# Recurrence units of four and three chunks cut at the dense groups, attention blocks counted by themselves

## The chip, the cores and the metric

The kernel runs on one core of one Trainium2 chip. The metric is the device time of one execution in microseconds (us). TensorE (PE) does the matrix products, PEld is its weight load, VectorE is DVE, ScalarE is ACT, GpSimd is POOL, and SyncE (SP) issues nearly all transfers. One profiled execution shows every instruction, its place in time and what ended the wait before it.

## What is computed

One layer of a decoder trunk runs over a prompt of 2048 tokens and 64 sample tokens, with model width 1024, all in float32. Cut to what matters:

```python
hn = rms_norm(x, g_pre_mix);  proj = hn @ w_in            # q, k, v of attention; r, k, v, decay, a, gate of RWKV
o_attn = sliding-window attention (window 128, 8 q heads, 2 kv heads, sinks)
def step(S, inp):                                         # RWKV-7, one token after the other
    sa = einsum('bhij,bhj->bhi', S, kk_t)
    S = S * w_t - sa (kk_t * a_t) + v_t k_t
    return S, einsum('bhij,bhj->bhi', S, r_t)
y = group_norm(ys) + bonus;  o_rw = y * g
mix = concat([o_attn, o_rw]) @ w_out;  x = x + rms_norm(mix)
f = (silu(conv3(z)) * u) @ w_ffn_out  with  z, u = rms_norm(x) @ w_ffn_in;  x = x + rms_norm(f)
```

## The kernel before

**Dense work.** The 2112 tokens are cut into five groups of columns: 448, 448, 448, 448 and 320 (`groups`, `GW`). For each group g there are stages: `P[g]` (`project`, 20 weight tiles), `O[g]` (`outproj`, 8 tiles) and two for the ConvFFN (`ffn`: 60 tiles, then a last one of 6), which stand in the list `F` as `F[2g]` and `F[2g+1]`. A tile's work is called a task here. It is 24 matmuls, since each product is made from two halves of either operand: `xhi·wh`, `xlo·wh`, `xhi·wl` (L182). For each task ACT writes `wh` (L351) and DVE writes `wl` (L352) out of the weight tile `w`. The stages run in the order of the list `order`:

P0 P1 P2 O0 P3 F0 O1 F1 P4 F2 O2 F3 O3 F4 F5 O4 F6 F7 F8 F9

**Side work.** Norms, the element-wise part of the projection (`shift`, `pair`, `rotary`) and what follows a stage (`rest`, L835 to L844 and L939 to L941) are generators. They are stepped between dense matmuls.

**Mixer.** The recurrence is done in chunks of 64 tokens (32 of them), the attention in blocks of 128 tokens (16 of them). A unit (`Mixer.unit`) is four chunks and two blocks, 256 tokens, so there are eight, and one more for the sample tokens. The recurrence of a unit goes through these steps:

- `scores`: for each chunk the matmuls `sc_e`, `sc_o`, and two DVE products with a mask (L1003) that make the tile `G`;
- `invert`: 31 steps on DVE, two instructions each (L1041, L1042), on all chunks of the unit at once (16 partitions to a chunk). Then an ACT copy (L1045), two stores that SP issues (L1050 is one), loads, and the matmuls `pz`;
- `chain`: chunk after chunk the matmuls `vt`, `bkt`, `pc`, `pu`, `pS`, with the state carried on;
- `groupnorm` on tiles of two chunks, `finish` (`pt`, `pg`), and the store of the result.

The attention of a unit (`attend`) runs beside it: `sc` and L1266, softmax (L1230 to L1241), `ppt`, `po`.

**What sets the order.** `Flow` keeps a planned clock that each emitted matmul moves on. After each dense matmul group `tick` lets at most one side step and one mixer step follow. A unit has a window from `start` to `end` in planned dense time; while the mixer's planned cost so far is over its share of `UNIT` (48e3), it is not stepped. A stage whose condition is not met is forced: `force` steps sides and mixer, without dense work between, until it is. `O[g]` needs the recurrence and attention of all units that touch its tokens: with groups of 448 and units of 256, `O0` needs units 0 and 1 (512 tokens), `O1` four units, `O2` six, `O3` seven. All engines take their instructions in the order in which they were emitted.

## Time and profile before

| | us |
|---|---|
| median of three runs | 2909.87 (2905.41 to 2914.93) |
| the profiled execution, its own time | 2909.42 |
| span of the profiled execution | 2907.6 |
| PE busy in the span | 2772.0 |
| DVE busy in the span | 1925.0 |
| ACT busy in the span | 1409.1 |

The dense stages can be found in time by counting matmuls of `gm` and `pf`. P1 runs from 126.7 to 315.2 us, P2 to 513.6, O0 to 572.0, P3 to 748.1, F0 to 1149.2, O1 to 1188.9, F1 to 1247.4, P4 to 1350.7, F2 to 1746.1, O2 to 1790.4, F3 to 1835.1, O3 to 1890.6, F4 to 2261.8. No mixer work stands after F4. The granted clock has two values in this trace, 1.0 (2.4 GHz) and 0.5 (1.2 GHz) of full speed, so a stretch's mean tells how much of it ran at the lower one.

### The profile page before, as it was taken

Reading aid. Unit: us, or ns where it says so; the run is one execution under the profiler, and the core shown is the slowest. Engines: PE = TensorE matmul, PEld = TensorE weight load, DVE = VectorE, ACT = ScalarE, POOL = GpSimd, SP = SyncE. Lnnn points to the kernel's source line nnn. Section 1 sums busy time; section 2 is a strip of 40 time slices with the busy share of each in tenths; the row PEclk is TensorE's granted clock in tenths of the full one; section 3 lists DMA queues with packets and bytes.
Section 4 is the critical chain, followed back from the end, with each engine's and each line's share of the span. In section 5 each row is a group of like instructions: output and inputs, shape, how many; then the busy total and the mean of one; then the engine's idle time right before and its main releaser. Section 6 shows DMA issues by size and latency. Waiting matters only on the chain.

```text
span 2907.6 us, 46258 instructions
## 1 busy us (share of the span) xinstructions
PE 2772.0 (95%) x16993; PEld 2354.7 (81%) x16993; DVE 1925.0 (66%) x3792; ACT 1409.1 (48%) x2628; POOL 239.3 (8%) x519
## 2 busy tenths in 40 slices
PE   8997998989999999998999999899999999999997
PEld 6875776758778789776887898778989999999997
DVE  6884885686756655687665556965764764447666
ACT  6553545546564554454655434455333443334543
POOL 1010010010000000022000010000000001001111
PEclk9997999989999999998999999999999999999998
DMA  6665645746744343565544335664433553335443
GB/s 200 195 201 136 193 142 147 219 127 196 217 143 126 104 148 123 170 198 142 180 134 136 115 108 160 208 196 133 130 115 109 186 182 107 109 105 177 157 150 119
DMA packets 310529, 446.58 MB, mean 154 GB/s; under 512 B 118536, under 2 KB 238952, under 8 KB 310288
## 3 DMA queue, kind: packets, MB, share of 16 engines
q1 hardware_dynamic: 309872, 443.48, 49.5%
...
q14 instruction: 91, 0.75, 0.1%
q10 hardware_dynamic: 432, 0.16, 0.0%
HBM read 362.19 MB, written 76.97 MB: 151 GB/s over the span
## 4 chain that ended last, share of the span: by engine, by line
PE 75%; DVE 13%; DMA 5%; ACT 3%; issue 3%; SPq 1%; DVEq 0%; ACTq 0%
PE gm L182 46%; PE pf L182 16%; PE pc L182 3%; DVE wl L352 2%; PE po L182 2%; DVE tt L1042 1%; DVE tmp L1041 1%; PE pz L182 1%; PE ppt L186 1%; ACT wh L351 1%; PE sc L182 1%; PE pu L182 1%; DMA w<-in_w_all 1%; PE pS L182 1%; PE sc_e L182 1%
## 5 line engine op out<-in xcount | busy, mean ns | idle before, releaser
L182 PE MATMUL gm<-xhi,wh 128*128 128x448 f32 (+3 forms) x2880 | 1056.1, 369 | 44.2 <-ACT wh L351 18.9
L182 PE MATMUL gm<-xhi,wl 128*128 128x448 f32 (+3 forms) x2880 | 1042.1, 363 | 14.9 <-DVE wl L352 14.6
L182 PE MATMUL gm<-xlo,wh 128*128 128x448 f32 (+3 forms) x2880 | 1039.5, 362 | 4.5 <-DVE xlo L352 4.2
L351 ACT CAST wh<-w 128x1024 fp32r<-128x1024 f32 (+1 forms) x470 | 489.5, 1042 | 720.3 <-PE gm L182 332.8
L352 DVE TENSOR_TENSOR wl<-w,wh 128x1024 fp32r<-128x1024 f32 (+1 forms) x470 | 569.9, 1213 | 381.8 <-ACT wh L351 377.6
L182 PEld LDWEIGHTS gm<-xhi,wh 128*128 128x128 f32 (+2 forms) x2880 | 544.2, 189 | 131.4 <-issue 31.4
L182 PEld LDWEIGHTS gm<-xhi,wl 128*128 128x128 f32 (+2 forms) x2880 | 544.3, 189 | 73.6 <-DVE wl L352 21.0
L182 PEld LDWEIGHTS gm<-xlo,wh 128*128 128x128 f32 (+2 forms) x2880 | 545.3, 189 | 60.3 <-DVE xlo L352 10.6
L182 PE MATMUL pf<-hh,wh 128*128 128x448 f32 (+1 forms) x880 | 317.8, 361 | 3.8 <-DVE acc L908 2.9
L182 PE MATMUL pf<-hl,wh 128*128 128x448 f32 (+1 forms) x880 | 312.5, 355 | 0.6 <-DVE hl L352 0.6
L182 PE MATMUL pf<-hh,wl 128*128 128x448 f32 (+1 forms) x880 | 312.4, 355 | 0.2 <-DVE wl L352 0.2
L881 POOL COPY zcar<-zz 128x2 f32<-128x2 f32 x110 | 74.4, 676 | 1547.6 <-ACT zz L870 1547.6
L908 DVE TENSOR_TENSOR acc<-acc,pf 128x448 f32<-128x448 f32 (+1 forms) x200 | 117.3, 589 | 103.4 <-PE pf L182 102.7
L182 PEld LDWEIGHTS pf<-hh,wh 128*128 128x128 f32 x880 | 165.3, 188 | 23.6 <-DVE acc L908 4.9
L182 PEld LDWEIGHTS pf<-hh,wl 128*128 128x128 f32 x880 | 165.3, 188 | 12.7 <-issue 1.0
L182 PEld LDWEIGHTS pf<-hl,wh 128*128 128x128 f32 x880 | 165.5, 188 | 11.8 <-DVE hl L352 1.0
L877 DVE SCALAR_TENSOR_TENSOR c<-zz,c_cw,c 128x448 f32<-128x448 f32 (+1 forms) x220 | 140.8, 640 | 26.2 <-ACT c L871 24.1
L891 DVE TENSOR_TENSOR c<-c,gm 128x448 f32<-128x448 f32 (+1 forms) x110 | 65.0, 591 | 120.4 <-PE gm L182 94.3
L884 ACT ACTIVATE c<-c 128x448 f32<-128x448 f32 (+1 forms) x110 | 61.2, 557 | 126.5 <-DVE c L877 89.3
L1041 DVE TENSOR_TENSOR tmp<-gb,tt 64x31 f32<-64x31 f32 (+21 forms) x279 | 91.4, 328 | 3.6 <-DMA gb<-dgr 1.0
L1042 DVE TENSOR_TENSOR tt<-tt,tmp 64x31 f32<-64x31 f32 (+21 forms) x279 | 91.9, 329 | 2.8
L351 ACT CAST xhi<-r 128x448 fp32r<-128x448 f32 (+1 forms) x112 | 59.3, 542 | 70.8 <-DMA r<-od 25.8
...
## 6 DMA issues: line engine op xcount, KB each, us to landing
w<-in_w SPq DMA_DIRECT2D x220, 512.0 KB
...
```

The lines of the kernel that those rows point to most:

```text
L182: return self.te.matmul(out, lhsT, rhs, **kw)
L186: return self.te.transpose(*args)
L351: self.nc.scalar.copy(out=hi, in_=src)
L352: self.nc.vector.tensor_tensor(out=lo, in0=src, in1=hi.bitcast(F32), op=ALU.subtract)
L877: v.scalar_tensor_tensor(out=c[:, :npr], in0=z[:, j:j + npr], scalar=cw(j), in1=c[:, :npr], op0=ALU.mult, op1=ALU.add)
L881: nc.gpsimd.tensor_copy(out=sh.zcar[:, f, :], in_=z[:, npr:npr + 2])
L884: nc.scalar.activation(out=c, in_=c, func=AF.Silu)
L891: v.tensor_tensor(out=c, in0=c, in1=ps, op=ALU.mult)
L908: v.tensor_tensor(out=accs[c], in0=accs[c], in1=ps, op=ALU.add)
L1041: v.tensor_tensor(out=tm, in0=col, in1=row, op=ALU.mult)
L1042: v.tensor_tensor(out=tt[:nb, w:, 0:w], in0=tt[:nb, w:, 0:w], in1=tm, op=ALU.subtract)
```

## The change

The prompt's recurrence is cut into nine units of 4, 3, 4, 3, 4, 3, 4, 4 and 3 chunks, so that units end at chunks 7, 14 and 21, which are the ends of the dense groups 0, 1 and 2. (The end of group 3, chunk 28, lies inside the eighth unit.) The attention blocks go with the units as 2, 2, 2, 1, 2, 2, 2, 1, 2, and each block has a token of its own: `O[g]` now needs the units that begin before its end and the blocks up to it. The `need` of a step is worked out from its own last token: attention block 3 waits for P1, while the unit of chunks 4 to 6 waits for P0 alone. The planned cost of a unit is `CHUNK` a chunk and `BLOCK` a block in place of `UNIT`, and the starts of the windows are moved. Three chunks leave a last tile of 64 rows in `chain`, `groupnorm` and `finish`.

```diff
-UNIT = 48e3
+CHUNK, BLOCK, SAMPLE = 7.3e3, 9.3e3, 48e3
...
-            if self.mixed - m0 > UNIT * (self.clock.t - self.mixed - start) / max(end - start, 1.0):
+            if self.mixed - m0 > cost * (self.clock.t - self.mixed - start) / max(end - start, 1.0):
...
-    def chain(self, c0, Gs, ys):
+    def chain(self, c0, n, Gs, ys):
...
-        for c in range(NC_):
+        for c in range(n):
             if c % 2 == 0:
+                m = min(2, n - c)
...
-    def unit(self, u, need):
+    def unit(self, u, c0, n, blocks, need):
...
         def attention():
-            yield lambda: need <= self.done
-            yield from self.attend(NB * u)
-            yield from self.attend(NB * u + 1)
-            self.flow.post(lambda: self.done.add(("A", u)))
+            for b in blocks:
+                w = need(128 * (b + 1))
+                yield lambda: w <= self.done
+                yield from self.attend(b)
+                self.flow.post(lambda b=b: self.done.add(("A", b)))
 
         def recurrence():
-            yield lambda: need <= self.done
+            w = need(CH * (c0 + n))
+            yield lambda: w <= self.done
...
+UNITS = [(4, 2), (3, 2), (4, 2), (3, 1), (4, 2), (3, 2), (4, 2), (4, 1), (3, 2)]
...
-        O = [dn.outproj(g, {(x, u) for u in range(-(-ends[g] // T)) for x in "AR"} | ({("S", 0)} if gs[g][2] else set())) for g in range(ng)]
+        O = [dn.outproj(g, {("R", u) for u, (c0, _, _) in enumerate(units) if CH * c0 < ends[g]} | {("A", b) for b in range(-(-ends[g] // 128))}
+                        | ({("S", 0)} if gs[g][2] else set())) for g in range(ng)]
...
-        windows = [(f(P[1], 0), f(P[1], 1)), (f(P[2], 0), f(P[2], 0.9)), (f(P[3], 0.1), f(F[0], 0.15)), (f(F[0], 0.15), f(F[0], 0.53)),
-                   (f(F[0], 0.53), f(F[0], 0.93)), (f(F[2], 0), f(F[2], 0.47)), (f(F[2], 0.47), f(F[2], 0.93)), (f(F[4], 0), f(F[4], 0.5))]
...
-        flow.units.append((f(F[4], 0.5), f(F[4], 0.93), [mx.sample({("P", ng - 1)})]))
+        starts = [f(*x) for x in ((P[1], 0), (P[1], 0.75), (P[2], 0.6), (P[3], 0.4), (F[0], 0.15), (F[0], 0.5), (F[2], 0), (F[2], 0.35),
+                                  (F[2], 0.7))]
+        need = lambda t: {("P", g) for g in range(ng) if gs[g][0] < t}
+        for u, (x, y, (c0, n, bs)) in enumerate(zip(starts, starts[1:] + [f(F[4], 0.35)], units)):
+            flow.units.append((x, y, CHUNK * n + BLOCK * len(bs), mx.unit(u, c0, n, bs, need)))
+        flow.units.append((f(F[4], 0.35), f(F[4], 0.9), SAMPLE, [mx.sample({("P", ng - 1)})]))
```

**First place: PE, the last tasks of P2.** The rows are the kernel before; `gm` is a dense matmul, `pt` and `pg` are the `finish` of unit 1, `sc` is attention of unit 2.

```order
L182 MATMUL gm<-xlo,wh 128x448
L182 MATMUL gm<-xhi,wl 128x448
L182 MATMUL pb<-b_4964,c_blockones 128x448
L186 MATMUL pt<-c_ident,y 128x128
L182 MATMUL pg<-sg,c_g_up 128x256 x2
L186 MATMUL pt<-c_ident,y 128x128 x7
L182 MATMUL pg<-sg,c_g_up 128x256 x2
L182 MATMUL sc<-kx,q 128x256 x4
L182 MATMUL gm<-xhi,wh 128x448 x2
```

The kernel after has the two halves of that `finish` apart; these are the rows around the first half, PE, in the last task but one of P2.

```order
L182 MATMUL gm<-xlo,wh 128x448
L182 MATMUL gm<-xhi,wl 128x448
L186 MATMUL pt<-c_ident,y 128x128
L182 MATMUL pg<-sg,c_g_up 128x192 x2
L182 MATMUL gm<-xhi,wh 128x448
```

Before, both halves stand between two dense matmuls of the 20th task, in which the chain of unit 1 also ends; now that chain ends in the 17th task, the first half stands in the 19th and the second in the 20th, and 30 dense matmuls lie between the halves.

**Second place: DVE, the middle of O3.** The rows are the kernel before; `acc` is the `rest` of F3, `tmp` and `tt` are the inversion of unit 7, `m`, `nm`, `es`, `den` its softmax, `wl` a weight half that the dense matmuls of O3 need.

```order
L939 SCALAR_TENSOR_TENSOR acc<-acc,c_gT,rb 128x448
L1041 TENSOR_TENSOR tmp<-gb,tt 64x252
L941 TENSOR_TENSOR acc<-acc,r 128x448
L1042 TENSOR_TENSOR tt<-tt,tmp 64x18x14
L1232 TENSOR_SCALAR nm<-m 128x4
L1233 TENSOR_TENSOR es<-c_sink,m 128x4
L1041 TENSOR_TENSOR tmp<-gb,tt 64x255
L769 TENSOR_TENSOR sa<-sa,sq 128x448
L1042 TENSOR_TENSOR tt<-tt,tmp 64x17x15
L352 TENSOR_TENSOR wl<-w,wh 128x1024
```

The kernel after, DVE, the same end of that `rest` in O3.

```order
L941 TENSOR_TENSOR acc<-acc,r 128x448
L939 SCALAR_TENSOR_TENSOR acc<-acc,c_gT,rb 128x448
L941 TENSOR_TENSOR acc<-acc,r 128x448
L769 TENSOR_TENSOR sa<-sa,sq 128x448
L941 TENSOR_TENSOR acc<-acc,r 128x448
L352 TENSOR_TENSOR wl<-w,wh 128x1024
```

Before, all 31 inversion steps of unit 7 stand in O3 and the first two tasks of F4; now the last prompt unit's stand in F2 (the 45th to the 51st of 60 tasks), and O3 has none.

**Third place: DVE, the middle of P3.** The rows are the kernel before; `L`, `b` and `tha` are the projection's `pair`, `s` and `G` are attention and scores of unit 3.

```order
L712 TENSOR_SCALAR L<-L 128x448
L713 SCALAR_TENSOR_TENSOR L<-scanm,L 128x448
L1266 SCALAR_TENSOR_TENSOR s<-sc,c_amask 128x512 x2
L728 SCALAR_TENSOR_TENSOR b_7486<-tha,e_7487 128x448
L1003 TENSOR_TENSOR G<-sc_e,c_wkmask 128x4x128
L1003 TENSOR_TENSOR G<-sc_o,c_wkmask 128x4x128
```

The kernel after, DVE, in the second half of P3.

```order
L1041 TENSOR_TENSOR tmp<-gb,tt 48x207
L677 SCALAR_TENSOR_TENSOR v<-h,c_vec,hm 128x448
L1042 TENSOR_TENSOR tt<-tt,tmp 48x23x9
L712 TENSOR_SCALAR L<-L 128x448
L1041 TENSOR_TENSOR tmp<-gb,tt 48x220
L713 SCALAR_TENSOR_TENSOR L<-scanm,L 128x448
L1042 TENSOR_TENSOR tt<-tt,tmp 48x22x10
```

Before, the inversion of unit 2 stands in the first seven tasks of P3, among the `rest` of O0; now unit 2's stands from the fifth task of O0 to the second of P3, and the one that shares P3's second half with the pairs is unit 3's, of three chunks (48 partitions), from the 14th task of P3 to the third of F0.

## Rows read from the trace of the kernel before

**Rows 1.** The page's first part: busy us, share of the span, instructions.

```profile
PE 2772.0 (95%) x16993; PEld 2354.7 (81%) x16993; DVE 1925.0 (66%) x3792; ACT 1409.1 (48%) x2628; POOL 239.3 (8%) x519
```

**Rows 2.** Windows: start:end, width, busy PE, PEld, DVE, ACT, POOL, clock, DMA, GB/s.

```profile
226.00:283.00 57.00, 40.26 (x324) 29.46 (x323) 25.01 (x52) 22.90 (x48) 1.80 (x8) 0.73 0.48 126
384.70:431.00 46.30, 43.57 (x205) 35.36 (x204) 44.98 (x117) 21.03 (x45) 7.60 (x12) 1.00 0.45 132
483.30:523.20 39.90, 28.78 (x128) 19.71 (x129) 26.21 (x62) 15.39 (x28) 1.99 (x5) 0.70 0.59 174
521.00:636.00 115.00, 96.72 (x485) 77.87 (x484) 92.19 (x232) 59.80 (x135) 6.01 (x13) 0.93 0.61 182
748.10:1149.20 401.10, 396.30 (x2680) 330.16 (x2679) 246.86 (x507) 206.39 (x388) 28.70 (x47) 1.00 0.44 135
1188.90:1247.40 58.50, 45.94 (x232) 37.88 (x230) 52.04 (x121) 26.63 (x65) 0.31 (x2) 0.91 0.62 196
1247.40:1386.30 138.90, 123.84 (x775) 101.54 (x776) 104.56 (x258) 70.65 (x164) 32.15 (x65) 0.90 0.59 171
1790.40:1835.10 44.70, 43.43 (x241) 34.10 (x239) 43.47 (x103) 22.40 (x46) 1.10 (x2) 1.00 0.62 191
1835.10:1953.80 118.70, 106.99 (x707) 84.49 (x706) 94.49 (x226) 62.92 (x128) 3.75 (x5) 0.91 0.62 197
2322.00:2622.30 300.30, 299.58 (x1461) 271.88 (x1462) 164.28 (x241) 122.47 (x178) 25.83 (x43) 1.00 0.40 128
```

**Rows 3.** Timeline of PE in P3: dense matmuls on either side of a clock change.

```profile
611.33 0.57 PE L182 MATMUL gm<-xhi,wh 128*96 128x448 f32 x1
611.70 0.57 PE L182 MATMUL gm<-xlo,wh 128*96 128x448 f32 x1
...
612.69 0.36 PE L182 MATMUL gm<-xlo,wh 128*96 128x448 f32 x1
612.89 0.36 PE L182 MATMUL gm<-xhi,wl 128*96 128x448 f32 x1
```

**Rows 4.** Timeline of PE at the end of P2.

```profile
497.36 1.83 PE L182 MATMUL pb<-b,c_blockones 128*128 128x448 f32 x2 [5.36 <-DVE rsg L53]
...
503.24 0.90 PE L186 MATMUL pt<-c_ident,y 128*128 128x128 f32 x3 [1.02 <-DVE y L1194]
```

**Rows 5.** Timeline of DVE in O3.

```profile
1872.97 0.67 DVE L939 SCALAR_TENSOR_TENSOR acc<-acc,c_gT,rb 128x448 f32<-128x448 f32 x1
1873.56 0.40 DVE L1041 TENSOR_TENSOR tmp<-gb,tt 64x252 f32<-64x252 f32 x1
...
1876.11 1.21 DVE L352 TENSOR_TENSOR wl<-w,wh 128x1024 fp32r<-128x1024 f32 x1
```

**Rows 6.** Timeline of PE at the same moment.

```profile
1877.37 0.74 PE L182 MATMUL gm<-xhi,wl 128*128 128x448 f32 x1 [7.42 <-DVE wl L352]
```

**Rows 7.** Groups on DVE: line, form, count, busy us, mean ns, idle before.

```profile
L1041 DVE TENSOR_TENSOR tmp<-gb,tt 64x31 f32<-64x31 f32 (+21 forms) x279 | 91.4, 328 | 3.6 <-DMA gb<-dgr 1.0
L1042 DVE TENSOR_TENSOR tt<-tt,tmp 64x31 f32<-64x31 f32 (+21 forms) x279 | 91.9, 329 | 2.8
L1003 DVE TENSOR_TENSOR G<-sc_e,c_wkmask 128x512 f32<-128x512 f32 x32 | 21.8, 682 | 8.8 <-PE sc_o L182 6.6 <-PE sc_e L182 2.1
L1230 DVE TENSOR_REDUCE m<-s 128x4 f32<-128x1024 f32 (+1 forms) x32 | 37.6, 1174 | 0.1
L1266 DVE SCALAR_TENSOR_TENSOR s<-sc,c_amask 128x512 f32<-128x512 f32 (+1 forms) x64 | 41.4, 662 | 13.5 <-PE sc L182 13.5
```

**Rows 8.** Waits of SP at an inversion's end: total us, times, longest.

```profile
SPq L1050 <- DVE tt L1042: 23.9, 8, 17.8
```

**Rows 9.** Waits of ACT at an inversion's end: the same columns.

```profile
ACT gb L1045 <- DVE tt L1042: 14.3, 5, 7.9
```

**Rows 10.** Groups on PE of the transposes of `finish` and `chain`.

```profile
L186 PE MATMUL pt<-c_ident,y 128*128 128x128 f32 x64 | 12.0, 297 | 3.6 <-DVE y L1194 2.4 <-ACT fin L1214 1.1
L186 PE MATMUL vt<-c_ident,vl 128*128 128x128 f32 x64 | 11.1, 299 | 0.0
```

More of the change, by code (lines that the diff above doesn't have):

```diff
@@ L239, in mixer @@
         if not self.mix and self.units:
-            start, end, gens = self.units[0]
+            start, end, cost, gens = self.units[0]
             if self.clock.t - self.mixed >= start or now == math.inf:
@@ L243, in mixer @@
                 self.mix = [Stream(g) for g in gens]
-                self.span = max(start, self.clock.t - self.mixed), end, self.mixed
+                self.span = max(start, self.clock.t - self.mixed), end, self.mixed, cost
         ready = [s for s in self.mix if s.at <= now and s.cond()]
@@ L259, in tick @@
         if self.mix:
-            start, end, m0 = self.span
-            if self.mixed - m0 > UNIT * (self.clock.t - self.mixed - start) / max(end - start, 1.0):
+            start, end, m0, cost = self.span
+            if self.mixed - m0 > cost * (self.clock.t - self.mixed - start) / max(end - start, 1.0):
                 return
@@ L1142, in chain @@
         yield 5000
-        for c in range(NC_):
+        for c in range(n):
             if c % 2 == 0:
+                m = min(2, n - c)
                 pv = self.ps("vt")
                 for p in range(4):
-                    te.transpose(pv[:, 128 * p:128 * p + 128], V[:, p], sh.ident)
-                for i in range(2):
+                    te.transpose(pv[:CH * m, 128 * p:128 * p + 128], V[:, p, :CH * m], sh.ident)
+                for i in range(m):
                     uvs[c + i] = self.t2("uv", tag="uv", bufs=2)
@@ L1154, in chain @@
             yield 1500
-            if c + 1 < NC_:
+            if c + 1 < n:
                 nxt = self.factors(c0 + c + 1)
@@ L1290, in attend @@
             yield 1000
-    def unit(self, u, need):
-        sh, nc, a = self.sh, self.nc, self.a
-        c0 = NC_ * u
+    def unit(self, u, c0, n, blocks, need):
+        sh, a = self.sh, self.a
         def attention():
-            yield lambda: need <= self.done
-            yield from self.attend(NB * u)
-            yield from self.attend(NB * u + 1)
-            self.flow.post(lambda: self.done.add(("A", u)))
+            for b in blocks:
[3 more added lines that the diff above has]
+                self.flow.post(lambda b=b: self.done.add(("A", b)))
         def recurrence():
-            yield lambda: need <= self.done
+            w = need(CH * (c0 + n))
+            yield lambda: w <= self.done
             Gs, ys = [], []
-            for c in range(NC_):
+            for c in range(n):
                 yield from self.scores(c0 + c, sh.wkmask, Gs)
             yield from self.invert(Gs)
-            yield from self.chain(c0, Gs, ys)
-            for y in ys:
-                yield from self.groupnorm(y)
-            yield from self.finish(ys, T, T * u)
-            if c0 + NC_ == sh.nch:
+            yield from self.chain(c0, n, Gs, ys)
+            for i, y in enumerate(ys):
+                yield from self.groupnorm(y, min(128, CH * n - 128 * i))
+            yield from self.finish(ys, CH * n, CH * c0)
+            if c0 + n == sh.nch:
                 self.store(a["o_wkv"], sh.S[self.si])
@@ L1621, in program @@
             sh.stacks(lambda name: mx.b4([128, D], name, "G"))
-        gs, nu = groups(seq), seq // T
+        gs = groups(seq)
         ng = len(gs)
@@ L1626, in program @@
         ends = [min(t0 + n, seq) for t0, n, _ in gs]
-        O = [dn.outproj(g, {(x, u) for u in range(-(-ends[g] // T)) for x in "AR"} | ({("S", 0)} if gs[g][2] else set())) for g in range(ng)]
+        units = []
+        for n, bs in UNITS:
+            c0, b0 = (units[-1][0] + units[-1][1], units[-1][2][-1] + 1) if units else (0, 0)
+            units.append((c0, n, range(b0, b0 + bs)))
+        O = [dn.outproj(g, {("R", u) for u, (c0, _, _) in enumerate(units) if CH * c0 < ends[g]} | {("A", b) for b in range(-(-ends[g] // 128))}
+                        | ({("S", 0)} if gs[g][2] else set())) for g in range(ng)]
         F = [f for g in range(ng) for f in dn.ffn(g)]
@@ L1635, in program @@
         f = lambda s, x: at[id(s)][0] + x * s.cost()
-        windows = [(f(P[1], 0), f(P[1], 1)), (f(P[2], 0), f(P[2], 0.9)), (f(P[3], 0.1), f(F[0], 0.15)), (f(F[0], 0.15), f(F[0], 0.53)),
-                   (f(F[0], 0.53), f(F[0], 0.93)), (f(F[2], 0), f(F[2], 0.47)), (f(F[2], 0.47), f(F[2], 0.93)), (f(F[4], 0), f(F[4], 0.5))]
-        for u, (x, y) in enumerate(windows):
-            need = {("P", g) for g in range(ng) if gs[g][0] < T * (u + 1)}
-            flow.units.append((x, y, mx.unit(u, need)))
-        flow.units.append((f(F[4], 0.5), f(F[4], 0.93), [mx.sample({("P", ng - 1)})]))
+        starts = [f(*x) for x in ((P[1], 0), (P[1], 0.75), (P[2], 0.6), (P[3], 0.4), (F[0], 0.15), (F[0], 0.5), (F[2], 0), (F[2], 0.35),
[4 more added lines that the diff above has]
+        flow.units.append((f(F[4], 0.35), f(F[4], 0.9), SAMPLE, [mx.sample({("P", ng - 1)})]))
         flow.run(dn.run(order))
```

4 lines of the change are left out of this document (2 added, 2 removed).

## The prediction, made before the changed kernel ran

> **What bounds the kernel now.** I read the page's busy times first. PE is busy for 2772.0 of 2907.6 us, DVE for 1925.0, ACT for 1409.1 [rows 1], so PE sets the time, and only 135.6 us of it are idle. But a busy PE can be a slow one. In P3 the same dense matmuls follow each other every 0.37 us (611.33, 611.70) and a moment later every 0.20 us (612.69, 612.89) [rows 3]; the first two ran at the lower clock of 1.2 GHz. So I price a stretch's loss as its idle time of PE plus (1 - granted clock) times its width: the time at the lower level is twice (1 - clock) of the width, and about half of it would be saved at the higher one. By the windows [rows 2], each cut at dense tasks, that gives
>
> - u0: 226.0 to 283.0, P1, end of unit 0's inversion: 16.7 + 0.27 x 57 = 32.1
> - A: 483.3 to 523.2, last task of P2 to the second of O0: 11.1 + 0.30 x 39.9 = 23.1
> - B: 521.0 to 636.0, O0 to the seventh task of P3: 18.3 + 0.07 x 115 = 26.3
> - C: 1188.9 to 1247.4, F1: 12.6 + 0.09 x 58.5 = 17.8
> - D: 1247.4 to 1386.3, P4 and two tasks of F2: 15.1 + 0.10 x 138.9 = 29.0
> - E: 1835.1 to 1953.8, O3 and the first tasks of F4: 11.7 + 0.09 x 118.7 = 22.4
>
> The six hold 151 us. F0, with two whole units mixed in, loses 4.8 us in 401, and F6, with none, 0.7 in 300 [rows 2]. So the amount of mixer work costs little beyond its own time on PE; what costs is where it meets side work on DVE, ACT and SP.
>
> Next I read who ends the waits. In A, PE stands 5.36 and 1.02 us behind small DVE instructions of the group norm [rows 4], because O0 is forced and nothing dense lies between. In E, inversion steps alternate with the `rest` of F3, and a `wl` behind them arrives 7.42 us late for PE [rows 5, 6]. At the end of an inversion, ACT and SP wait in line with it: SP up to 17.8 us before the store L1050, ACT up to 7.9 before the copy L1045, 14.3 in five cases [rows 8, 9]; weight loads and `wh` queue behind them.
>
> DVE being nearly full is not itself a loss: F3 has DVE busy 43.5 of 44.7 us and loses 1.3; the stretch of unit 1's inversion, 384.7 to 431.0, has 45.0 of 46.3 and loses 2.7 [rows 2]. It becomes one when DVE gets more than PE in the same tasks, or many inversion steps at once.
>
> **The change part by part.** I counted in both orders what stands in each dense task and priced it with the group means; sums of many small groups below are such estimates.
>
> *Work added.* One more inversion: 62 DVE instructions, (91.4 + 91.9) / 9 = 20.4 us, as a step's price is that of its columns [rows 7]. It falls into F2, where like F0 (DVE 247 of 401 us) there is room, so I put it at nothing; without that cover it costs up to 20. On PE the tiles of 64 rows bring 16 more `pt` and 16 more `vt` records, at 12.0 / 64 and 11.1 / 64 us [rows 10] at most 5.8, at least 0 where they overlap neighbours; I take **+3**.
>
> *A, end of P2.* O0 needs chunks to 7 in place of 8. Unit 1 starts in the same place, but its chain ends three tasks earlier and the two halves of its `finish` get dense work between. Between the 17th task of P2 and the second of O0, PE has some 12 us less (chain matmuls) and DVE some 12 more: unit 2's scores, softmax and two splits come in. DVE is late next, by about 7 us over PE. So of 23.1 between 7 and all remain; I take 10, the lower end with a little of the group norm's chain: **-13** (-16 to 0).
>
> *B, O0 and P3.* Unit 2's inversion moves from among O0's `rest` in P3 into O0, where DVE had room, and its chain (PE work, some 24 us) comes to stand beside that `rest`. DVE gets about 5 us more in B, 97 in all, while PE's work goes from 97 to 121, so PE leads. Unit 1's row says 3 may remain, B itself 26; I take 14: **-12** (-23 to 0).
>
> *E, O3.* The inversion, a block's softmax and scores leave, a chunk and a half and two group norms come: DVE -18, PE -10. DVE then has about 77 us beside some 97 of PE. Nearest is F3, which loses 1.3; with the group norm's small steps now inside O3 I take 8 of 22.4: **-14** (-21 to -5).
>
> *D, P4.* Unit 6 stands where unit 5 stood, but all its scores, and one block's attention more, now fall into P4: six more L1003, four L1266, two L1230 [rows 7] are 4.1 + 2.6 + 2.3, and half a `pair` comes in, 15 us of DVE in all, with 9 of PE that have left F4. DVE leads, so the stretch grows by up to 15, of which 9 are moved, not new: **+6** (-5 to +15).
>
> *End of P3 and F0.* Unit 3's inversion now meets the projection's pairs. The rows nearest are unit 0's and unit 1's, both among pairs: 32.1 and 2.7. Unit 0 has 13 of its 31 steps in one dense task, unit 1 two to five a task in the second half; unit 3 has two to five. So I take unit 1's side: **+4** (2 to 32).
>
> *C, F1.* The next stage waits for the norm of P4, which waits for the `rest` of O1; no unit is involved, so the force stays. Unit 5's chain adds 2 us of DVE: **+2** (-5 to +8). Its PE work fills idle time that is there in both. O1, O2, F2 take over what F4 loses, at PE's price: 0.
>
> *u0.* The same instructions stand there, 14 steps in the one task for 13: 0 (-10 to +5). After F4 nothing differs.
>
> A side look at the price of a loss. In E, PE is busy for 90% of the width, its weight load for 84.49 of 118.7 us; in F6 for 271.88 of 300.3 [rows 2]. The Trainium skill, Perfetto Trace Analysis, "Identifying the Most-Contended Engine", says that matmul busy time is no measure of the distance to the limit, and to take the share of weight loads. With F6's share of 0.905 as full, A, B and E lose 18.1 + 29.0 + 25.3 = 72.4, against 71.8 by my price and 41.1 by idle time alone. By that rule the sum stays; by idle alone the three gains shrink to about 22 us and the time is 2902.
>
> **Sum.** -13 - 12 - 14 + 6 + 4 + 2 + 3 = **-24 us**. The profiled execution took 2909.42 us, 1.8 over its span, and stands within 0.5 of the median of 2909.87. So 2909.9 - 24 = **2886**.
>
> **The rivals.**
>
> - *The inversion blocks ACT and SP among the pairs (slower).* Unit 3's inversion at the end of P3 and unit 6's in P4, with eight steps in P4's last task, hold up `wh` and the weight loads as unit 0's does. Price: the end of P3 costs 32 in place of 4, D 15 in place of 6, so -24 + 28 + 9 = +13: 2923. It decides from the point where SP waits longer than some 10 us at L1050, as it does once now (17.8), and PE for `wh`. For it: the largest of the six losses is of this kind. Against: unit 1 does the same work among pairs for 2.7.
> - *Waits of latency, not of load (no change).* A's and E's small chains are as long as before and only stand elsewhere: unit 1's group norm before O0, unit 8's inside O3, the `rest` of O0 before F0. Then A gives 5, B 4, E 7, and the additions of 15 stay: -1, 2909. For it: DVE gains 20 us in all, and P2 and P4 get more of it. Against: between the halves there is now dense work, and 30 matmuls at 0.20 us cover 6 us, more than the 5.36 of the worst wait.
> - *The additions are hidden (larger gain).* D, C and the end of P3 at nothing: -39 + 3 = -36, 2874. With A, B and E near their lower ends too it would be below 2860.
>
> **How the numbers follow.** I give the forecast 0.48, the hidden additions 0.14, the waits of latency 0.21, the blocked queues 0.17. Faster means below 2901, since about 0.3% is what a measurement of this kernel can tell from no change; the first two cases are there but for their edges, where a gain shrinks to a few us: 0.62. Within 0.3%: the third: 0.22. Slower: 0.16. The range takes in the hidden additions with half of what A, B and E could still give, and most of the case of no change: 2862 to 2914. The blocked queues and the far low end are left out.
>
> **What the changed kernel's profile would show.** Right: at the end of P2 no wait of 5 us behind `rsg` and a clock near 1; in O3 no `tmp`, `tt`, and no `wl` 7 us late; the first seven tasks of P3 at a clock above 0.9. P4 longer than 103.3 us by 5 to 15, F4 shorter by some 30. Wrong: a wait of PE for `wh` at the end of P3 or of P4 with SP standing before L1050; F1 longer than 65 us; O0 stretched by unit 2's inversion, so that B only moves forward; u0 changed by more than 10 us, which would mean that small differences in order decide and not the loads counted here.

## The result and the profile after

The kernel after takes 2894.47 us (median of 11 runs, 2889.23 to 2902.03), the kernel before beside it 2910.14 us. The ratio is 0.9944, with a 95% interval of 0.9934 to 0.9954: 15.7 us faster. The forecast was 24 us, 2886 us, with a range of 2862 to 2914. The sign and the range hold, the gain is two thirds of the forecast.

The profiled execution of after took 2902.03 us, the longest of its 11 runs. Its difference to the profile of before (7.4 us) is therefore smaller than that of the medians, and a few us in one stage are not to be read from the two traces alone. That is why steps A, B and E are also tested by runs that undo them.

The page's first part of after, to be read beside [rows 1]: the added inversion is 62 of the 100 instructions that DVE has more (3892 for 3792), and PE is busy for 6.1 us more.

```profile
PE 2778.1 (96%) x17017; PEld 2375.4 (82%) x17017; DVE 1954.9 (67%) x3892; ACT 1413.9 (49%) x2635; POOL 266.2 (9%) x521
```

The windows of after, cut at the same dense tasks as [rows 2] (start:end, width, busy PE, PEld, DVE, ACT, POOL, granted clock, DMA share, GB/s). In order: u0, A, B, F0, C, D, E.

```profile
229.20:292.50 63.30, 44.33 (x392) 31.27 (x391) 26.20 (x54) 25.22 (x55) 2.68 (x6) 0.76 0.52 141
490.65:525.47 34.82, 26.46 (x116) 19.40 (x115) 28.77 (x62) 15.31 (x40) 2.03 (x1) 0.81 0.74 222
525.47:664.42 138.95, 129.35 (x935) 98.99 (x934) 96.86 (x232) 78.89 (x178) 6.69 (x15) 0.90 0.61 186
751.20:1152.40 401.20, 395.79 (x2679) 332.07 (x2679) 259.01 (x536) 209.65 (x395) 37.95 (x49) 0.99 0.45 135
1199.90:1261.00 61.10, 47.79 (x304) 39.10 (x302) 52.25 (x141) 28.23 (x65) 0.31 (x2) 0.85 0.58 184
1261.00:1412.10 151.10, 136.75 (x877) 109.79 (x876) 118.49 (x290) 78.58 (x187) 29.31 (x69) 0.91 0.59 175
1862.30:1948.50 86.20, 85.28 (x539) 73.45 (x539) 76.66 (x164) 50.56 (x92) 5.49 (x13) 1.00 0.68 220
```

With the price of the prediction, PE's idle time plus (1 - clock) times the width:

| stretch | before | forecast change | after | change read |
|---|---|---|---|---|
| u0 | 32.1 | 0 | 34.2 | +2.1 |
| A | 23.1 | -13 | 15.0 | -8.1 |
| B | 26.3 | -12 | 23.5 | -2.8 |
| end of P3 and F0 (F0's loss) | 4.8 | +4 | 9.4 | +4.6 |
| C | 17.8 | +2 | 22.5 | +4.7 |
| D | 29.0 | +6 | 28.0 | -1.0 |
| E | 22.4 | -14 | 0.9 | -21.5 |

The changes add up to -22, with PE's 6 us of further busy time -16. That this lies beside the -15.7 of the medians is chance. The table is read from two executions that differ by 7.4 us, PE's 6 us hold time at the lower clock, which the price has already counted, and outside the seven stretches the price rose. Two places show it, before and then after: from u0 to A, and from the end of E to the end of F4.

```profile
283.00:483.30 200.30, 192.33 (x1395) 145.31 (x1393) 144.37 (x315) 106.80 (x233) 17.57 (x38) 0.98 0.57 166
1953.80:2261.80 308.00, 307.94 (x1835) 270.89 (x1834) 190.24 (x339) 131.09 (x214) 25.02 (x49) 1.00 0.40 125
```

```profile
292.50:490.65 198.15, 189.15 (x1244) 146.10 (x1243) 146.39 (x340) 107.39 (x228) 25.64 (x44) 0.95 0.54 154
1948.50:2256.30 307.80, 304.82 (x1664) 269.44 (x1663) 181.74 (x315) 122.36 (x192) 24.46 (x41) 0.98 0.40 122
```

Between u0 and A the loss goes from 12.0 to 18.9, in F4 from 0.1 to 9.1. In the whole span the price falls by about 2 us only (PE's idle time from 135.6 to 122.2, the mean clock from 0.973 to 0.969). The first of the two places belongs to step A: the chain of unit 1, which now ends earlier, stands in P2 from 445.5 to 463.1 us without a dense matmul, and the clock is at 0.5 from 453.9 to 467.6. So from the end of u0 to the second task of O0 PE loses 33.9 for 35.1: nearly all that A gains is lost just ahead of it.

In the table B stands out: forecast as the second largest gain, it gave nearly nothing, though PE leads there as foreseen (129 us busy beside DVE's 97). Half of what B loses is clock: 10.2 us at 0.5 between O0 and P3, with waits of 2.17 and 2.48 us for the norm, and 17.1 us in P3.

What happens in P3 is seen in PE's timeline in task 3 of P3 (start, us, engine, line, operation, count, idle time before and what ended it):

```profile
612.93 1.07 PE L182 MATMUL po<-pT,va 128*64 128x512 f32 x2 [0.31 <-ACT pT L1280]
...
615.40 0.72 PE L182 MATMUL pz<-G,zt 32*32 32x32 f32 x16 [0.86 <-ACT zt L1071]
616.04 0.66 PE L186 MATMUL vt<-c_ident,vl 128*128 128x128 f32 x4
...
617.58 1.80 PE L182 MATMUL pc<-S,ab 64*128 64x64 f32 x14
619.31 1.12 PE L182 MATMUL pc<-uv,G 64*64 64x64 f32 x16
620.88 1.51 PE L182 MATMUL pu<-rhs,G 64*64 64x64 f32 x16 [0.45 <-ACT rhs L1111]
...
629.76 1.51 PE L182 MATMUL pu<-rhs,G 64*64 64x64 f32 x16 [0.45 <-ACT rhs L1111]
631.23 0.74 PE L182 MATMUL gm<-xhi,wh 128*128 128x448 f32 x1
```

Between 608.6 and 631.2 no dense matmul runs: most of the `pz` of unit 2 and of the chain of two chunks stand in one row. I call such a row a **bunch** below. The windows on either side of the clock change, and a second case in F0 (task 4, unit 3):

```profile
608.64:617.80 9.16, 7.27 (x107) 4.38 (x107) 1.53 (x3) 5.33 (x17) 0.00 (x0) 1.00 0.50 158
617.80:634.90 17.10, 15.74 (x168) 13.46 (x167) 6.29 (x11) 9.19 (x22) 0.70 (x2) 0.50 0.74 243
785.00:795.20 10.20, 9.22 (x95) 7.33 (x92) 1.92 (x3) 5.69 (x13) 0.00 (x0) 0.50 0.64 191
```

The clock falls to 1.2 GHz after 9 us in which PE was busy for 7.3, without a wait above 0.86 us, and stays there for 17 us in which it is busy for 15.7. DVE is busy for less than 40% of each of the three rows. The Trainium skill, TensorE: Matmul & The Clock Gate, "Why this matters for your kernels", puts a fall of the clock in mid-kernel down to idle gaps of PE between bursts of matmuls. The wait of 5.36 us at the end of P2 before, with the clock of A at 0.70 [rows 2, 4], agrees; ahead of 617.80 there is no such gap, so here the trace shows a fall that this rule doesn't tell.

**Where the bunches come from**, and a correction: the part on the kernel before says that the engines take instructions in the order of emission. That is inexact. Between emission and the queues stands the framework's scheduler, which may hold an instruction back and gives those emitted earlier the precedence once they are ready. The plan spreads the mixer steps over the tasks, but the pauses in `invert` amount to a few us, while on DVE the inversion takes some 40. Its `pz` and chain are therefore emitted long before it is done, and where it ends they go ahead of the dense work. I read this from the order; the run with pauses below tests the remedy, not the scheduler's inner reason. Nor does it tell why the change made more bunches: the kernel before has the same pauses, and of the 2576 matmuls of the chain that are listed with that run, 60 start at the lower clock there, 386 in after (counted in the traces). That stays open.

### The profile page after: what moved, and what is told of

Its sections match the earlier page's. It is cut to its first block, busy times and chain, and to the rows that moved or that the text cites. A ratio compares the mean times of both kernels' runs of the same rounds, so it can differ in the third digit from the quotient of the medians.

```text
span 2900.2 us, 46428 instructions
## 1 busy us (share of the span) xinstructions
PE 2778.1 (96%) x17017; PEld 2375.4 (82%) x17017; DVE 1954.9 (67%) x3892; ACT 1413.9 (49%) x2635; POOL 266.2 (9%) x521
## 4 chain that ended last, share of the span: by engine, by line
PE 82%; DVE 8%; DMA 4%; ACT 3%; issue 2%; SPq 0%; POOL 0%; DVEq 0%; ACTq 0%; POOLq 0%
PE gm L182 50%; PE pf L182 17%; PE pc L182 3%; PE po L182 1%; DVE wl L352 1%; DMA r<-x2d 1%; PE sc L182 1%; PE ppt L186 1%; PE sc_e L182 1%; PE pz L182 1%; PE pu L182 1%; ACT wh L351 1%; DVE tt L1042 1%; DVE tmp L1041 1%; PE ms L182 1%
## 5 line engine op out<-in xcount | busy, mean ns | idle before, releaser
L182 PEld LDWEIGHTS gm<-xhi,wh 128*128 128x128 f32 (+2 forms) x2880 | 543.4, 189 | 115.4 <-issue 23.9
L1041 DVE TENSOR_TENSOR tmp<-gb,tt 64x31 f32<-64x31 f32 (+37 forms) x310 | 102.5, 331 | 5.0 <-DMA gb<-dgr 0.6
L1042 DVE TENSOR_TENSOR tt<-tt,tmp 64x31 f32<-64x31 f32 (+37 forms) x310 | 102.9, 332 | 4.4
```

The source lines that it names most:

```text
L182: return self.te.matmul(out, lhsT, rhs, **kw)
L1041: v.tensor_tensor(out=tm, in0=col, in1=row, op=ALU.mult)
L1042: v.tensor_tensor(out=tt[:nb, w:, 0:w], in0=tt[:nb, w:, 0:w], in1=tm, op=ALU.subtract)
```

## The experiments

All ratios are to the kernel before (after: 0.9944); a difference of two ratios has an uncertainty of about 0.0015 to 0.0022, 4 to 6 us.

### A undone: O0 needs eight chunks again

```diff
-UNITS = [(4, 2), (3, 2), (4, 2), (3, 1), (4, 2), (3, 2), (4, 2), (4, 1), (3, 2)]
+UNITS = [(4, 2), (4, 2), (3, 2), (3, 1), (4, 2), (3, 2), (4, 2), (4, 1), (3, 2)]
```

> The kernel after with one cut moved back: units of 4, 4, 3, 3, 4, 3, 4, 4, 3 chunks, so that O0 needs eight chunks again while O1 and O2 keep their new needs, and all else stays. My theory of the prediction (a force before O0 that has a chunk less to finish is shorter, and that is what A gained: 23.1 us of loss before, 15.0 after): A returns, +8 to +13 us on the kernel after (2894.5), so 2902 to 2908, with the 5 us wait behind rsg back at the end of P2. Rival (what costs is that the matmuls pz, pc, pu, pS of a unit stand in one bunch behind its inversion, and a cut only moves the bunches): the sum of bunches is as large in this order as in the kernel after, so -4 to +4, 2890 to 2898.

Measured: 2906.75 us, ratio 0.9983 (0.9971 to 0.9994), 11 us over the kernel after. PE's timeline and the window of A in this run:

```profile
501.69 1.83 PE L182 MATMUL pb<-b,c_blockones 128*128 128x448 f32 x2 [5.36 <-DVE rsg L53]
...
507.57 0.90 PE L186 MATMUL pt<-c_ident,y 128*128 128x128 f32 x3 [1.03 <-DVE y L1195]
```

```profile
487.62:532.38 44.76, 33.33 (x171) 22.49 (x169) 31.58 (x73) 17.46 (x37) 2.23 (x5) 0.73 0.61 186
```

The wait of 5.36 is back to the hundredth [rows 4], and A loses 11.4 + 12.1 = 23.5 for 23.1 before. So the mechanism of step A is shown in its stretch. The size is not: the run also moves the bunches of units 1 to 3. From u0 to A, and in F0, its windows are

```profile
292.40:487.62 195.22, 188.65 (x1323) 142.89 (x1323) 141.57 (x313) 106.28 (x230) 16.14 (x40) 0.98 0.56 163
750.95:1160.00 409.05, 401.89 (x2684) 338.73 (x2683) 257.81 (x519) 209.07 (x396) 25.12 (x49) 0.97 0.45 134
```

a loss of 10.5 for after's 18.9, and of 19.4 for 9.4; B loses 17.1 for 23.5. How much of the 11 us is A's own stays open.

### E alone: the last units of before moved into F2

```diff
-        ... (f(F[2], 0), f(F[2], 0.47)), (f(F[2], 0.47), f(F[2], 0.93)), (f(F[4], 0), f(F[4], 0.5))]
+        ... (f(F[2], 0), f(F[2], 0.35)), (f(F[2], 0.35), f(F[2], 0.7)), (f(F[2], 0.7), f(F[4], 0.35))]
...
-        flow.units.append((f(F[4], 0.5), f(F[4], 0.93), [mx.sample({("P", ng - 1)})]))
+        flow.units.append((f(F[4], 0.35), f(F[4], 0.9), [mx.sample({("P", ng - 1)})]))
```

> The kernel before (2910) with its eight units of four chunks, where only the windows of the last units are moved: units 5, 6 and 7 start at 0, 0.35 and 0.7 of F2 and the sample at 0.35 of F4, as the kernel after has it, so that no inversion falls into O3. My theory (step E of the prediction: an inversion beside the rest of F3 in O3 costs 22 us there, in F2 next to nothing; the cutting of units has no part in it): -14 to -21 us, 2889 to 2896. Rival (moved, not saved: P4 and F2 grow by what O3 and F4 lose): 2905 to 2914. Should this kernel alone come to the time of the kernel after, the cuts at 7, 14 and 21 would bring nothing.

Measured: 2889.68 us, ratio 0.9922 (0.9910 to 0.9935): 22.7 us off, a little more than theory E gave. This is the net of a trade: in the profiles O2 to F4 lose 2.5 for 23.9 before, P4 and F2 36.9 for 30.4. The run is also 6 us better than the whole change (uncertain by 5), so all the rest of it together costs more than it gains.

### Counting blocks alone

The code of after with the windows of before and eight units:

```diff
-UNITS = [(4, 2), (3, 2), (4, 2), (3, 1), (4, 2), (3, 2), (4, 2), (4, 1), (3, 2)]
+UNITS = [(4, 2)] * 8
```

> The code of the kernel after with eight units of four chunks and the windows of before: only the attention blocks have their own tokens and needs, and the cost is counted by chunk and block (47.8e3 a unit in place of 48e3). All theories: no chunk or block is needed earlier or later by a stage than its unit was, but for blocks 3, 7 and 11, so within 0.3% of before, 2904 to 2918. If it is slower than before, the counting of blocks is a part of the 17.7 us by which the change falls short of its gains.

Measured: 2908.64 us, ratio 0.9981 (0.9971 to 0.9991), 5.5 us faster than before (uncertain by 3). The prediction gave this part no price, and I have no row that tells where it lies.

### E undone in the kernel after

```diff
-        starts = [... (F[2], 0), (F[2], 0.35), (F[2], 0.7))]
+        starts = [... (F[2], 0), (F[2], 0.47), (F[4], 0))]
```

with the sample at 0.5 of F4.

> The kernel after (0.9944) with the end of the row as before: unit 7 starts at 0.47 of F2, unit 8 at 0 of F4 (by the planned clock, which puts its inversion into O3 and the first tasks of F4 again), the sample at 0.5 of F4; units 0 to 6 as in the kernel after. Theory (step E, an inversion beside the rest of F3 in O3 costs what it cost before, whatever the cutting): +14 to +22 us, 0.999 to 1.002. Rival (with units of three chunks a smaller inversion and chain come there, or F2 with a unit less gains as much as O3 loses): 0 to +8, 0.9944 to 0.997.

Measured: 2903.13 us, ratio 0.9973 (0.9958 to 0.9987): 8.4 us over the kernel after. That is the rival's number, at its edge. The windows of this run (E, P4, F2), then those of P4 and F2 of after:

```profile
1832.56:1946.16 113.60, 99.98 (x531) 78.71 (x531) 94.29 (x219) 57.28 (x113) 1.69 (x5) 0.92 0.59 189
1260.06:1361.32 101.26, 99.73 (x627) 86.52 (x627) 92.74 (x209) 59.05 (x137) 27.25 (x64) 0.98 0.69 209
1361.32:1739.50 378.18, 371.62 (x2515) 318.18 (x2514) 227.94 (x436) 190.19 (x337) 28.35 (x54) 0.99 0.44 134
```

```profile
1260.99:1376.64 115.65, 107.09 (x637) 90.19 (x636) 106.68 (x266) 60.75 (x146) 26.74 (x66) 0.96 0.61 184
1376.64:1779.30 402.66, 395.02 (x2709) 333.14 (x2708) 257.09 (x516) 206.61 (x383) 29.57 (x54) 0.98 0.46 138
```

In its place the loss is back in full (13.6 + 9.1 = 22.7, for 0.9). But P4 loses 3.5 for 13.2 and F2 10.3 for 15.7: the units are a queue, and the last one can only stand earlier if those ahead of it crowd into P4 and F2. So E and D are one trade: 21.8 gained, 15.1 paid, 6.7 net in the profiles and 8.4 by the medians.

### B undone in the kernel after

```diff
-        starts = [... (P[2], 0.6), (P[3], 0.4), (F[0], 0.15), (F[0], 0.5), ...]
+        starts = [... (P[3], 0.1), (F[0], 0), (F[0], 0.2), (F[0], 0.55), ...]
```

> The kernel after (0.9944 of before) with unit 2 put back: it starts at 0.1 of P3 as before, units 3, 4 and 5 at 0, 0.2 and 0.55 of F0, the end of unit 1 kept. So the inversion of unit 2 stands in tasks 1 to 5 of P3 beside the rest of O0 (before: 0 to 6; after: from O0's fifth task to P3's second), its chain behind it. Theory of the prediction (B: that place costs 12 us more than O0 with the chain in P3): 0.9944 + 0.0041, 0.9985, +12 us. What the profile of after suggests instead (B lost 23.0 for 26.3, as the bunch of unit 2's matmuls took the place of the inversion): +3 us, 0.995. If the inversion in O0 is itself a loss (O0 took 72.4 us for 58.3), it comes out faster, 0.990 to 0.993.

Measured: 2897.47 us, ratio 0.9949 (0.9935 to 0.9964): 1.5 us over the kernel after, within the uncertainty of nothing. Its windows of A, B and P4:

```profile
489.42:513.64 24.22, 21.94 (x76) 15.16 (x75) 16.92 (x32) 10.37 (x19) 0.60 (x1) 0.79 0.70 214
513.64:636.88 123.24, 102.27 (x517) 80.41 (x515) 94.85 (x235) 60.03 (x137) 5.51 (x13) 0.89 0.59 169
1269.79:1378.74 108.95, 105.92 (x635) 89.86 (x635) 102.61 (x252) 60.30 (x145) 32.98 (x65) 0.96 0.63 188
```

B loses 34.5 for 23.5, but A 7.4 for 15.0 and P4 7.4 for 13.2. The place matters here too, and most of it is given back elsewhere, in A with the scores of unit 2 gone from the force before O0. The net gain of 12 is not there.

### The inversion's end taken off ACT and SP

The copy of L1045 on GpSimd; the stores, the loads back and the `zt` loads from GpSimd's queue.

```diff
-        nc.scalar.copy(out=xx[:nb], in_=tt[:nb].rearrange("q s t -> q t s"))
+        nc.gpsimd.tensor_copy(out=xx[:nb], in_=tt[:nb].rearrange("q s t -> q t s"))
...
-        nc.sync.dma_start(out=dx[:nb, :], in_=xx[:nb].rearrange("q s t -> q (s t)"))
+        nc.gpsimd.dma_start(out=dx[:nb, :], in_=xx[:nb].rearrange("q s t -> q (s t)"))
```

> The kernel after with the end of every inversion taken off ACT and SP: the copy of L1045 is done by GpSimd, and the two stores, the loads back and the zt loads are issued from GpSimd's queue. In the kernel after SP stands 19.5 us before L1050 in P1 and ACT 7.9 us before L1045, then PE 8.7 us for wh; the stretch from 229.2 to 292.5 loses 34 us. Rival of the prediction (the inversion blocks the queues of ACT and SP): these 34 us shrink by 15 to 20, elsewhere a few more, -15 to -25 us on the kernel after, 2870 to 2880. Bunch theory: 128 pz in one task of P1 stay in a bunch and keep the clock low there for 20 us, only the wait of 8.7 can go: -8 to 0, 2887 to 2895, or slower where GpSimd's copies are long.

Measured: 2919.35 us, ratio 1.0024 (1.0008 to 1.0040): 23 us slower than the kernel after, worse than either theory's numbers. The stretch u0, and PE's waits for `zt` (total us, times, longest) in this run and in after:

```profile
230.14:288.08 57.94, 44.32 (x391) 31.33 (x390) 26.66 (x53) 23.81 (x54) 20.71 (x33) 0.76 0.53 146
```

```profile
PE pz L182 <- DMA zt<-dtr: 27.9, 10, 5.7
```

```profile
PE pz L182 <- DMA zt<-dtr: 3.0, 3, 1.5
```

u0 loses 27.5 for 34.2: the blocked queues are worth 7 us there, not 15 to 20, and the clock is no better. The remedy brings a worse wait, for the `zt` loads from the new queue. The Trainium skill, DMA: Bandwidth & Descriptors, "Issuing engine by pattern", calls the queues of SP and ACT generally faster than GpSimd's; this run agrees in sign, with 27.9 us of waiting for 3.0, but does not show it alone: GpSimd's own copy of L1045, of 2.1 to 3.1 us, stands in the same queue ahead of the stores.

### Pauses in the inversion: the bunches taken apart

The kernel after, with the same instructions; from the third unit on, and for the sample:

```diff
-            if j and j % 4 == 0:
-                yield 1500
+            if j and j % (4 if self.early else 2) == 0:
+                yield 1500 if self.early else 5000
...
+            self.early = c0 < 7
             yield from self.invert(Gs)
```

> The kernel after, where from the third unit on (and for the sample) the generator of the inversion asks for more planned time: every second of its 31 steps a pause of 5000 in place of every fourth one of 1500. No instruction is added or removed; the matmuls behind an inversion (pz, chain) are emitted later and thereby get a later place among the dense ones. In the kernel after they stand in bunches of 8 to 14 us in single dense tasks (counted from 0: P3 tasks 3 and 4, F0 tasks 4 and 20, F2 tasks 1 and 26, F4 task 24), and PE loses 40 us in these tasks, mostly at the lower clock. Bunch theory: with the bunches gone most of these 40 us come back, -20 to -35 us on the kernel after, 2860 to 2875, and no drop of the clock at the ends of these inversions. Theory of DVE load, that of the prediction: DVE's work near these places stays as it is, so the loss stays, -5 to +5, 2890 to 2900.

Measured: 2866.95 us, ratio 0.9844 (0.9831 to 0.9856): 29 us faster than the kernel after and 45 faster than before. The bunch theory holds in its number. That the clock no longer falls at the ends of these inversions holds but for one place, in B. The page's first part and the windows of B (from O0's second task to P3's eighth) and F0:

```profile
PE 2755.8 (96%) x17017; PEld 2353.5 (82%) x17017; DVE 1957.8 (68%) x3892; ACT 1412.2 (49%) x2633; POOL 248.2 (9%) x521
```

```profile
522.41:642.19 119.78, 110.84 (x683) 83.15 (x682) 89.40 (x213) 68.83 (x152) 7.05 (x15) 0.94 0.63 189
742.29:1125.20 382.91, 381.30 (x2556) 321.13 (x2555) 262.48 (x547) 192.24 (x354) 25.78 (x47) 1.00 0.44 135
```

PE is busy for 22 us less with the same 17017 instructions. The clock accounts for about as much: (1 - clock) times the span is 89.9 us in after (0.969 of 2900.2) and 68.7 here (0.976 of 2863.1). B now loses 8.9 + 7.2 = 16.1, close to the 14 of the forecast; most of its lost clock stands behind one wait of PE, at whose end the clock is at 0.5, until 632.0:

```profile
621.35 0.28 PE L182 MATMUL pz<-zt,G 32*32 32x32 f32 x2 [4.15 <-DMA zt<-dtr]
```

F0 loses 1.6 for 9.4, with 18 us less width; of this some 6 us are mixer work that has moved on (123 records fewer, at about 50 ns). DVE does as much as before, but the pauses also spread its inversion steps (those of unit 4 over 44 us for 36) and set them later, and this run does not part that from the bunches. For the bunches speaks F0: DVE has room there in both runs (259 of 401 us, 262 of 383), and the clock is back at 1.00. The whole of F4 loses 1.0 for 10.3. Where PE's time goes is in the groups of the chain's matmuls (count, busy us, mean ns, idle before): first the kernel before, then after, then this run.

```profile
L182 PE MATMUL pc<-uv,G 128*64 128x64 f32 (+1 forms) x1024 | 50.8, 227 | 0.0
L182 PE MATMUL pc<-S,ab 64*128 64x64 f32 x512 | 38.4, 283 | 0.0
L182 PE MATMUL pu<-rhs,G 64*64 64x64 f32 x528 | 26.0, 228 | 0.0
L182 PE MATMUL pS<-uv,bkt 128*64 128x64 f32 x512 | 25.8, 230 | 0.0
```

```profile
L182 PE MATMUL pc<-uv,G 128*64 128x64 f32 (+1 forms) x1024 | 60.3, 237 | 0.0
L182 PE MATMUL pc<-S,ab 64*128 64x64 f32 x512 | 43.7, 300 | 0.5 <-DVE S L1172 0.5
L182 PE MATMUL pS<-uv,bkt 128*64 128x64 f32 x512 | 30.8, 240 | 1.5 <-ACT uv L1119 1.4
L182 PE MATMUL pu<-rhs,G 64*64 64x64 f32 x528 | 30.2, 245 | 1.7 <-ACT rhs L1111 1.7
```

```profile
L182 PE MATMUL pc<-uv,G 128*64 128x64 f32 (+1 forms) x1024 | 51.7, 232 | 0.0
L182 PE MATMUL pc<-S,ab 64*128 64x64 f32 x512 | 39.9, 292 | 0.5 <-DVE S L1174 0.5
L182 PE MATMUL pu<-rhs,G 64*64 64x64 f32 x528 | 26.6, 236 | 0.4 <-ACT rhs L1113 0.4
L182 PE MATMUL pS<-uv,bkt 128*64 128x64 f32 x512 | 26.2, 234 | 0.5 <-ACT uv L1121 0.5
```

The same 2576 records take 141.0 us before, 165.0 after and 144.4 with pauses. The change made bunches, and with them these four groups take 24 us more. Of the records 60, 386 and 208 start at the lower clock.

### Pauses on eight units, on all units, on unit 1

The kernel of the run E alone, with the diff of the pauses above:

> The kernel before with the last units moved into F2 (2889.7 us) and, from the third unit on and for the sample, the pauses of 5000 at every second step of the inversion. It differs from the kernel with nine units and the same pauses (2867.0) by the cuts alone: eight inversions in place of nine, and eight chunks for O0 in place of seven. Theory A (the cuts cost 17.7 us beside what A gains, because a ninth unit brings a ninth bunch and the cuts moved bunches into P3 and the start of F0 and F2; with the bunches gone they cost only their work, about 3 us on PE): slower than nine units by 5 to 9 us, 2872 to 2876, as A's 11 us are missing. Theory B (a ninth unit costs by itself, through 20 us more of DVE): faster than nine units by 4 to 8 us, 2859 to 2863. In either case faster than 2889.7 by 14 us or more if bunches cost in this kernel too.

Measured: 2880.53 us, ratio 0.9884 (0.9866 to 0.9902), 11 us less than without pauses; in the kernel of nine units they gain 29. So without pauses nine units are 6 us worse than eight with the same last windows (0.9944 and 0.9922), with pauses 12 better (0.9844 and 0.9884). In the profiles with pauses P2 and O0 lose 32.0 us with nine units for 40.8 with eight, P3 16.5 for 21.9. Theory A holds: its 5 to 9 us lie within the uncertainty of the 12, and theory B, by which nine would be slower, is not borne out. What the cuts cost goes with the bunches.

The first two units too:

```diff
-                yield 1500 if self.early else 5000
+                yield 4000 if self.early else 5000
```

> As the kernel with the pauses of 5000, and the first two units too get pauses of 4000 in place of 1500 (every fourth step). In the kernel after their bunches stand in P1 tasks 15 and 16 and P2 tasks 15 and 16, where PE loses 36 us, of which the wait for the inversion's end in P1 (8.7) is not the bunch's. Bunch theory: another -5 to -15 us on the run with pauses from the third unit on, less what O0's force gains, since unit 1 ends later. Load theory: 0, or slower by 5 to 10 through the force before O0.

Measured: 2877.47 us, ratio 0.9878 (0.9863 to 0.9894), 10 us slower than with pauses from the third unit on. Load theory had this end: P1 takes 198.8 us for 194.6, P2 188.9 for 182.9.

Unit 1 alone of the first two (steps between pauses, length of one):

```diff
-            self.early = c0 < 7
+            self.pause = (4, 1500) if c0 < 4 else (4, 5000) if c0 < 7 else (2, 5000)
```

> The kernel of nine units with pauses from the third unit on (0.9844), where unit 1 alone gets longer pauses too: 5000 in place of 1500 at every fourth step; unit 0 keeps its own (the run with longer pauses in all units came out 10 us slower, 0.9878, with P1 4 and P2 6 us longer). The matmuls of unit 1 then stand in two smaller bunches of 7.5 and 9.6 us in P2's tasks 15 and 16 in place of one of 13.9, which with its follower lost 13 us. Bunch theory (a bunch costs in P2 as in F0, and what did harm was unit 0): -4 to -8 us, 0.9815 to 0.983. Rival (in the projections the pairs and the force before O0 set the end, a later chain only brings it nearer to O0): 0 to +8, 0.9844 to 0.987.

Measured: 2860.79 us, ratio 0.9812 (0.9795 to 0.9830), the best of all: 1.9% or some 54 us faster than the kernel before, and 9 us faster than without the pause in unit 1 (uncertain by 6). The sign is that of the bunch theory, but its place in P2 is not shown: up to the end of F0 the two profiles stand at 1124.8 and 1125.2 us.

### Other places for the units

The kernel with pauses from the third unit on, with other starts:

```diff
-        starts = [... (P[2], 0.6), (P[3], 0.4), (F[0], 0.15), (F[0], 0.5), (F[2], 0), (F[2], 0.35), (F[2], 0.7))]
+        starts = [... (F[0], 0.1), (F[0], 0.32), (F[0], 0.55), (F[0], 0.78), (F[2], 0.2), (F[2], 0.45), (F[2], 0.7))]
```

> The kernel of nine units with pauses (2867.0), where only the starts are moved: units 2 to 5 start at 0.1, 0.32, 0.55 and 0.78 of F0, units 6 to 8 at 0.2, 0.45 and 0.7 of F2, the end of unit 1 kept. So no inversion stands in O0 or beside the rest of O0 in P3, and few steps of one in P4. Theory of the prediction on places (B: mixer work beside the rest of O0 costs by DVE; D: units in P4 cost 5 to 15): P3, now 22.9 us over its work, falls to P0's 11 to 15, P4 by 5, and F0 and F2 take the work at its price: -10 to -18, 2849 to 2857. Bunch theory: without bunches the place matters little; -4 to +4, 2863 to 2871.

Measured: 2888.96 us, ratio 0.9911 (0.9893 to 0.9928), 19.5 us slower than with the units in their old places, which neither theory gave. From O0 to the end of F0, and from F3 to the end of O3; in each the first row of this run, the second of the run with pauses:

```profile
504.88:1078.00 573.12, 559.72 (x3411) 464.68 (x3411) 404.50 (x815) 299.40 (x559) 37.54 (x86) 0.99 0.53 159
1785.60:1894.10 108.50, 98.84 (x521) 79.57 (x521) 89.89 (x213) 51.64 (x99) 0.18 (x1) 0.91 0.61 190
```

```profile
503.81:1125.20 621.39, 602.90 (x3968) 493.54 (x3968) 447.99 (x963) 326.40 (x643) 42.11 (x88) 0.98 0.52 158
1790.30:1884.10 93.80, 91.64 (x648) 78.64 (x647) 75.59 (x149) 50.38 (x96) 1.98 (x9) 0.96 0.71 223
```

In O0, P3 and F0 the loss falls from 30.9 to 19.1, so the place does matter, as the prediction had it. But the last unit's inversion comes to stand in O2 and O3 again, and F3 and O3 lose 19.4 for 5.9: units put off are pushed into the next bad place.

The last unit past O3:

```diff
-        starts = [... (F[2], 0), (F[2], 0.35), (F[2], 0.7))]
+        starts = [... (F[2], 0), (F[2], 0.47), (F[4], 0.15))]
```

> The kernel of nine units with pauses (0.9844), the last unit moved past O3: unit 6 and 7 at 0 and 0.47 of F2, unit 8 at 0.15 of F4, where its inversion stands in tasks 1 to 12 with nothing beside it, the sample at 0.55 of F4. O3 needs only the units up to chunk 28, which is why the ninth can wait. Theory (a place costs by what stands beside it, F4 is empty, and F2, where the units crowd and lose 22 us in the run with pauses, gets one unit fewer): -5 to -12 us on 0.9844, 0.980 to 0.983. Rival (F2 is no bound, a unit costs its PE work wherever it stands): 0.984 to 0.986.

Measured: 2870.85 us, ratio 0.9860 (0.9842 to 0.9879); the difference of 5 us to 0.9844 is not more than its uncertainty. A unit fewer in F2 gains nothing that can be measured: the rival.

## Why the prediction was right in sign and short in size

- **The price of a stretch.** It finds where PE loses, but the sum over the forecast's stretches is no forecast of the whole: -16 beside -15.7 is luck, as some 20 us came up outside them. By idle time alone A, B and E go from 41.1 to 18.9, by the price from 71.8 to 39.4. The Trainium skill's measure (Perfetto Trace Analysis, "Identifying the Most-Contended Engine", the share of weight loads) gives 72.4 to 48.0. The three undoing runs give 21 us (11.4 + 1.5 + 8.4); the 22 of idle time are the nearest, then the 24 of weight loads, the 32 of the price are far. But each of these runs moved losses elsewhere too, so this does not decide which measure is right.
- **A: right in its stretch, not in what it is worth.** -8 in the profile, for -13. The 5.36 wait is gone with the halves of `finish` apart. But the chain that ends three tasks earlier stands there in a bunch, and the stretch ahead of A loses 18.9 for 12.0; the forecast had no term for it. The run's 11 us hold other moves too. At the granted clock I was wrong (0.81, not near 1): scores and attention of unit 2 now stand in the force before O0, and PE waits 3.99 us for `xhi` in O0.
- **B: the step that failed.** It said "PE leads. Unit 1's row says 3 may remain, B itself 26; I take 14". PE does lead, but I took a leading PE for one at full clock. Most of unit 2's matmuls came in one bunch, 17.1 us at 1.2 GHz, and 3 were gained for 12. With the bunch taken apart B stands at 16.1. The place, too, is worth less than forecast: back in P3, unit 2 costs B 11 us more and A 8 less.
- **The sentence behind it**, "the amount of mixer work costs little beyond its own time on PE; what costs is where it meets side work", is half wrong. It also matters whether the work stands in a bunch: in F0, with DVE at 259 of 401 us, the loss went from 4.8 to 9.4, and with pauses to 1.6.
- **Work added on PE, +3: short.** PE's busy time grew by 6.1 us, the four groups of the chain by 24.0. I had counted 32 records more, 16 `pt` and 16 `vt`; there are 24 (8 `pt`, 8 `vt`, 8 `pg`), since the 64-row tiles stand in place of full ones. What happens to the 2576 others had no term. The added inversion at nothing was right: with pauses nine units are no dearer than eight.
- **E and D: each mis-sized, as one trade.** E gave 21.5 for 14 in its stretch. But moving the last unit moves those ahead of it; in the kernel after the trade is worth 8, in the kernel of eight units 22.7. D's own change (-1 for +6) hides this, since D was compared with a layout that already had a unit there.
- **End of P3 and F0, +4: right size, other reason.** F0 grew by 4.6, and its one stretch at the lower clock (785.0 to 795.2) stands in the bunch of its task 4; no wait behind the pairs decides there.
- **C, +2:** 4.7 was read. **u0, 0:** 2.1. Both within their bounds; C not tested by a run.
- **Counted blocks:** no term; 5.5 us by the run.
- **The rivals.** Blocked queues: no. The end of P3 cost 4.6, not 32, and taking the queues away gained 7 in u0 and lost 23 in all. Latency, not load: no for E; for A its number (5) is as near to the 8 as the forecast's 13, though the wait that it meant is gone; for B its number (4) came out, by another mechanism. Hidden additions: no.
- **Signs.** Right: no wait behind `rsg`, no `wl` 7 us late in O3, P4 longer by 12, F4 shorter by 27. Not come: the first seven tasks of P3 ran at 0.85, not above 0.9. Of the wrong ones one came: O0 was stretched from 58.3 to 72.4 us, and B mostly moved forward.

Open: u0's 34 us, the largest loss left, which neither the queues nor pauses mended; where the 9 us of the pause in unit 1 lie, and why the cuts made more bunches.
